# One fp32 product in place of three products of rounded parts, in the time-mixing layer of a hybrid decoder step

## The chip, the cores and the metric

The kernel runs on one core of a Trainium2 chip. The metric is device microseconds of one execution, the median of three runs. The core has five engines with instruction streams of their own: TensorE (PE, whose weight loads are listed apart as PEld), VectorE (DVE), ScalarE (ACT), GpSimd (POOL) and SyncE (SP), which here issues most DMAs.

## The reference, cut to what matters

One inference step of two layers: a Conformer convolution layer and an RWKV-7 time-mixing layer, each followed by a squared-ReLU MLP. 1024 prompt tokens with 16 meta tokens ahead and 8 sampled tokens are computed, all in fp32, with a width of 1024 and 16 heads of 64. The change lies in the time-mixing layer:

```python
prev = concatenate([shift_prev, h[:, :-1]]);  xx = prev - h
xr, xw, xk, xv, xa, xg = (h + xx * x_mix[i] for i in range(6))
r, k, v = xr @ w_r, xk @ w_k, xv @ w_v                       # 1024 x 1024 each
w_log = -softplus(-(w0 + tanh(xw @ w1) @ w2)) - 0.5          # low rank: 64
a = sigmoid(a0 + (xa @ a1) @ a2)                             # low rank: 64
g = sigmoid(xg @ g1) @ g2                                    # low rank: 128
...
S_final, ys = lax.scan(_wkv7_step, S0, (r, decay, k, v, kk, a))
...
out = ((yn + bonus) * g) @ w_o
```

## The kernel before

Activations lie feature-major: 128 features on the partitions, KT = 8 blocks of features, tokens along the free dimension. The time-mixing layer takes the 1048 tokens in four groups (G1: 272, 256, 256 and 264 tokens) through `mixer_in`, while `prepare` of the next group runs between, and the recurrence over 17 chunks of 64 tokens (`chunk`, `front`) is let in piece by piece: `tick` is called at fixed places of the projections and gives the recurrence a credit (`PACE`). The Tile framework then orders the instructions of each engine by priority and by its own simulated times, so the order on an engine is not the order in the code; waits between engines are semaphores.

In a group the phases follow each other: `mixed(0)` makes the mixed input of r (eight tiles `mx`, on VectorE); eight projections of r; `gate`, the first low-rank product of g; the mixed input of k and eight projections of k, each followed by the second low-rank product of g (`lora2`, tile `l_g`) and a column of the norms of kk (`pn`); `decay_rate`, the first low-rank product of w and a together; the mixed input of v and eight projections of v, each with the second low-rank products of w and a (`l_w`, `l_a`), the cumulated decays (`cum`, part of the tile `wa`), the operands of the recurrence (`ab`) and, one tile later, `finish`, which stores `ab`, transposes v and makes the small products `nn` and `pk`.

Every one of these matrix products is made of three: both operands are split into a rounded part of type fp32r and the rest, and `mm3` adds high x high, low x high and high x low in PSUM:

```python
nc.tensor.matmul(ps, w[0], act[0], start=first, stop=False)   # L187
nc.tensor.matmul(ps, w[1], act[0], start=False, stop=False)   # L188
nc.tensor.matmul(ps, w[0], act[1], start=False, stop=last)    # L189
```

The weights come by DMA as columns of 128 (512 KB, `load_raw`, L146, on SyncE's queue). `load_w` casts them on ScalarE (`*_hi`, L157) and subtracts on VectorE (r, k and the first two of v) or on GpSimd (the rest of v, and the low-rank weights) (`*_lo`, L162). `col_stream` holds the order of the 96 columns of r, k and v: loads two columns ahead, the split one ahead. Activations are split by `split` (L140 on ScalarE, L141 on VectorE or GpSimd): `mx` into `mh` and `ml`, the input of the low-rank products `hx` into `hxh` and `hxl` (`input_parts`, let in beside the projections of r), the results of the first low-rank stage into `lgh`, `lgl` and the like. The first low-rank stage (`narrow`) has two weight blocks for each block of features, one for the token's own row and one for the row before it; in the last group the sampled tokens' rows before, `sps`, are put between the others.

The MLPs, the convolution layer's products and w_o use `mm3` as well and are not touched. Some products of the recurrence and its preparation take plain fp32 operands: `A` (L1209), `pk` (L1064), `pn` (L983) and others.

Of the kernel before, what the change touches and what calls it, by code (L numbers as in the profile page):

```python
# [16 lines left out]
P = 128  # L17
# [5 lines left out]
DEC = 8  # L23
# [25 lines left out]
def hybrid_step(tc, x_prompt, x_sample, state_conv, state_shift, state_wkv, meta_tokens,  # L49
# [10 lines left out]
    with ctx:  # L60
        def pool(stack, name, bufs, **kw):
            return stack.enter_context(tc.tile_pool(name=name, bufs=bufs, reuse_waits="tile", **kw))
# [699 lines left out]
        open_ep(ld, 1, "d")  # L762


        lwa = [[lorap.tile([P, N1], F32R, name=f"l{b}{q}") for q in "hl"] for b in "wa"]
        for i in range(2):
            for t in lwa[i]:
                nc.scalar.copy(t[HALF[1 - i]], hsel[HALF[1 - i], 0:1].broadcast_to([HS, N1]))

        prep = {}  # L770
        VSLOW = 0.5
        LO_R = LO_K = lambda p: nc.vector
        LO_V = lambda p: nc.vector if p < 2 else nc.gpsimd

        def prepare(g):

# [32 lines left out]

            def mix(i, k):  # L810

                t = tt(nm("mx", i, k), "t2")
                nc.vector.scalar_tensor_tensor(t[:, :n], xx[:, k, :n], vec("x_mix", i * KT + k), hx[:, k, 1:1 + n],
                                               op0=ALU.mult, op1=ALU.add)
# [6 lines left out]
        RAW_AHEAD, SPLIT_AHEAD = 2, 1  # L821
        wrkv = col_stream([(w, p, f"w{s}{g}_{p}", lo(p)) for g in range(4)
                           for s, w, lo in (("r", rwkv_w_r[0], LO_R), ("k", rwkv_w_k[0], LO_K), ("v", rwkv_w_v[0], LO_V))
                           for p in range(KT)], RAW_AHEAD, SPLIT_AHEAD)
        carry = {"tail": lambda: None}

        def mixer_in(g, tick, ahead):
# [34 lines left out]
            nl = n if npr == n else npr + 2 * DEC  # L862
            HK = KT // 2
            hxs = {}

            def input_parts():
                yield
                for hf in range(2):
                    hi = pr.tile([P, 5 * 4 * HS], F32R, name=nm("hxh", hf), tag="ab", bufs=2)
                    los = [pr.tile([P, 3 * N1], F32R, name=nm("hxl", hf, i), tag=tag, bufs=2) for i, tag in enumerate(("rk2", "wa"))]  # L870
                    for k in range(hf * HK, hf * HK + HK):
                        h_ = hi[:, k % HK * (1 + N1):(k % HK + 1) * (1 + N1)]
                        l_ = los[k % HK // 2][:, k % 2 * (1 + N1):(k % 2 + 1) * (1 + N1)]
                        srcs = [(slice(0, 1 + npr), hx[:, k, :1 + npr])]
                        if npr < n:
                            srcs += [(slice(1 + npr, 1 + nl, 2), sps[:, k]), (slice(2 + npr, 1 + nl, 2), hx[:, k, 1 + npr:1 + n])]
                        for cs, src in srcs:
                            split(h_[:, cs], l_[:, cs], src, nc.gpsimd)
                        hxs[k] = h_, l_
                        if k % 2:  # L880
                            yield

            def narrow_w(i, name):

                return [load_w(d_lr[i, :, hf * HK:(hf + 1) * HK].rearrange("p k s c -> p (k s) c"), (KT, P), nm(name, hf), nc.gpsimd)
                        for hf in range(2)]

            def narrow(ws, name):

                ps = bank(nm("p", name))[:, :nl]  # L890
                for k in range(KT):
                    w = ws[k // HK]
                    for s_ in range(2):
                        j = k % HK * 2 + s_
                        mm3(ps, (w[0][:, j, :], w[1][:, j, :]), [t[:, 1 - s_:1 - s_ + nl] for t in hxs[k]],
                            j == 0 and k == 0, j == KT - 1 and k == KT - 1)
                return ps


            ncols = [(slice(0, npr), slice(0, npr))] + ([(slice(npr, n), slice(npr + 1, nl, 2))] if npr < n else [])  # L900
            lo_ = lambda s: lorap.tile([P, N1], F32R, name=nm(s), tag=s)
            lg = lo_("lgh"), lo_("lgl")
            def decay_rate(ws):
                lf = lorap.tile([P, N1], F32, name=nm("lf"), tag="lf")
                ps = narrow(ws, "wa")
                for d, sc in ncols:
                    nc.scalar.activation(lf[:64, d], ps[:64, sc], AF.Tanh)
                    nc.scalar.copy(lf[64:, d], ps[64:, sc])
                for rows, (hi, lo) in zip(HALF, lwa):
                    split(hi[rows, :n], lo[rows, :n], lf[rows, :n], nc.gpsimd)  # L910

            def gate(ws):
                ps = narrow(ws, "g")
                lf2 = lorap.tile([P, N1], F32, name=nm("lf2"), tag="lf")
                for d, sc in ncols:
                    nc.scalar.activation(lf2[:, d], ps[:, sc], AF.Sigmoid)
                split(lg[0][:, :n], lg[1][:, :n], lf2[:, :n], nc.gpsimd)
# [15 lines left out]

            def second(parts, name):

                raw = cur["raw"].tile([P, D], F32, name=nm(name) + "_raw", tag="raw")
                for rows, src in parts:
                    nc.sync.dma_start(raw[rows], src)
                return load_w(None, (KT, P), nm(name), nc.gpsimd, raw=raw)

            dd = lambda p, i, src: nc.gpsimd.tensor_copy(ddec[:, p, i, :], src)
            allp = slice(0, P)
# [11 lines left out]


            act = mixed(0)
            aside = input_parts()
            both = beside(aside, (0, 1))
            for p in range(KT):
                (both if p else lambda: tick(1.0))()  # L960
                ps = proj(next(wrkv), act, P, f"r{p}", both if p else lambda: tick(1.0))
# [5 lines left out]
                nc.scalar.copy(r[:, :n], ps[:, :n])  # L967
# [5 lines left out]
            for _ in aside:  # L973
                pass
            gate(ws)
            act = mixed(2)
            both = lambda: tick(1.0)
# [23 lines left out]
            r16p = [lorap.tile([P, N1], F32R, name=nm("r16" + q), tag="lg" + q)[:, :n] for q in "hl"]  # L1001

            def norms():
                add_pn()
# [620 lines left out]
```

## Time and profile before

| | |
|---|---|
| median of 3 runs | 2857.89 us (2855.55 to 2860.58) |
| profiled execution, span | 2857.3 us; no other time of it is listed |
| mean granted TensorE clock | 0.961 |
| PE, DVE, ACT, POOL busy | 94%, 69%, 47%, 60% of the span |
| time-mixing projections, first to last matmul | 1126 to 1833 us from the span's start |

Times in the profile are of one execution. Matmuls are pipelined, and the durations of neighbouring ones overlap, so what one costs is read from the step between starts. A product of plain fp32 operands stands in the trace as two records, a product of fp32r operands as one. "Busy" counts the union of the durations. The granted clock (PEclk) is the share of the full TensorE clock that was granted.

### The profile page before, as it was taken

To read this page: it belongs to the slowest core of one execution; us is meant where nothing else is said; L and a number is where in the kernel's file an instruction comes from. 1 tells how busy PE (TensorE), PEld (TensorE's weight loads), DVE (VectorE), ACT (ScalarE), POOL (GpSimd) and SP (SyncE) were. 2 spreads that over 40 slices of the span, in tenths; PEclk is the share of its full clock that TensorE was granted. 3 is DMA by queue.
4 is the path that set the end of the run, shared out by engine and by line. 5 is a ranking of instruction groups with operands and counts; after the bars stand their busy time and mean duration, and the time that the engine had idled before them with its cause. 6 is when DMAs were issued, how large, how long until landed. Compare 5 with 4: busy or idle time off the path is not lost. (4 is left out here: it accounts for less than half of the span.)

```text
span 2857.3 us, 54445 instructions
## 1 busy us (share of the span) xinstructions
PE 2677.4 (94%) x20554; PEld 2557.9 (90%) x20554; DVE 1958.0 (69%) x3726; ACT 1345.6 (47%) x2510; POOL 1703.4 (60%) x2295
## 2 busy tenths in 40 slices
PE   8999999999999899878788899979999999999998
PEld 7989999999999898867787788778889999999998
DVE  5999999995455545478896895689656764443444
ACT  5545444543454334565666857634445552222223
POOL 6676877887788775444543554646448783333332
PEclk9999999999999999988899999989999999999999
DMA  6662544454444642777777968856557742222211
GB/s 179 172 184 85 159 135 133 133 179 140 136 129 148 176 138 91 215 194 198 202 215 208 241 165 198 234 156 159 128 161 213 205 128 85 70 72 67 67 60 41
DMA packets 659285, 428.34 MB, mean 150 GB/s; under 512 B 126840, under 2 KB 609208, under 8 KB 659022
## 3 DMA queue, kind: packets, MB, share of 16 engines
q1 hardware_dynamic: 652780, 421.93, 52.6%
q8 instruction: 162, 2.65, 0.4%
q10 hardware_dynamic: 6018, 2.89, 0.4%
q14 instruction: 101, 0.83, 0.1%
q0 software_dynamic: 224, 0.03, 0.0%
HBM read 353.03 MB, written 72.66 MB: 149 GB/s over the span
## 5 line engine op out<-in xcount | busy, mean ns | idle before, releaser
L162 POOL TENSOR_TENSOR wo_lo<-wo_raw,wo_hi 128x256 fp32r<-128x256 f32 x736 | 561.5, 795 | 300.3 <-ACT wo_hi L157 265.5
L162 POOL TENSOR_TENSOR wi_lo<-wi_raw,wi_hi 128x256 fp32r<-128x256 f32 x640 | 490.4, 797 | 275.5 <-ACT wi_hi L157 264.1
L187 PE MATMUL out<-hh,wo_hi 128*128 128x352 f32 (+2 forms) x1536 | 503.5, 328 | 20.1 <-DVE h L340 10.6
L340 DVE TENSOR_TENSOR h<-h,out 128x352 f32<-128x352 f32 (+2 forms) x768 | 386.3, 510 | 197.8 <-PE out L189 196.9
L187 PE MATMUL ps_in<-m_h,wi_hi 128*128 128x352 f32 (+2 forms) x1536 | 497.4, 324 | 12.2 <-ACT m_h L269 11.5
L189 PE MATMUL out<-hl,wo_hi 128*128 128x352 f32 (+2 forms) x1536 | 496.0, 325 | 4.0 <-DVE hl L141 4.0
L188 PE MATMUL out<-hh,wo_lo 128*128 128x352 f32 (+2 forms) x1536 | 499.4, 325 | 0.0
L188 PE MATMUL ps_in<-m_h,wi_lo 128*128 128x352 f32 (+2 forms) x1536 | 496.5, 324 | 0.0
L189 PE MATMUL ps_in<-m_l,wi_hi 128*128 128x352 f32 (+2 forms) x1536 | 496.2, 323 | 0.1
L504 DVE SCALAR_TENSOR_TENSOR cv<-u,wdw,cv 128x352 f32<-128x352 f32 (+2 forms) x720 | 377.3, 575 | 0.7
L157 ACT CAST wi_hi<-wi_raw 128x1024 fp32r<-128x1024 f32 x160 | 168.1, 1050 | 396.9 <-PE out L189 188.4
L157 ACT CAST wo_hi<-wo_raw 128x1024 fp32r<-128x1024 f32 x184 | 192.9, 1049 | 316.8 <-PE out L189 145.6
L187 PEld LDWEIGHTS out<-hh,wo_hi 128*128 128x128 f32 x1536 | 292.6, 191 | 27.5 <-DVE h L340 14.8
L187 PEld LDWEIGHTS ps_in<-m_h,wi_hi 128*128 128x128 f32 x1536 | 290.6, 189 | 14.6 <-ACT m_h L269 11.6
L189 PEld LDWEIGHTS out<-hl,wo_hi 128*128 128x128 f32 x1536 | 291.6, 190 | 6.4 <-DVE hl L141 5.3
L188 PEld LDWEIGHTS out<-hh,wo_lo 128*128 128x128 f32 x1536 | 292.5, 190 | 1.7
L188 PEld LDWEIGHTS ps_in<-m_h,wi_lo 128*128 128x128 f32 x1536 | 290.3, 189 | 2.0
L189 PEld LDWEIGHTS ps_in<-m_l,wi_hi 128*128 128x128 f32 x1536 | 289.9, 189 | 1.9 <-DVE m_l L270 0.5
L327 DVE SCALAR_TENSOR_TENSOR r<-ps_in,rs_m 128x352 f32<-128x352 f32 (+2 forms) x192 | 98.6, 516 | 232.7 <-PE ps_in L189 228.9
L141 DVE TENSOR_TENSOR hl<-s,hh 128x352 fp32r<-128x352 f32 (+2 forms) x192 | 144.5, 754 | 109.9 <-ACT hh L140 109.8
L329 ACT ACTIVATE s<-r 128x352 f32<-128x352 f32 (+2 forms) x192 | 93.7, 490 | 130.8 <-DVE r L327 130.3
L162 POOL TENSOR_TENSOR wv_lo<-wv_raw,wv_hi 128x256 fp32r<-128x256 f32 x96 | 82.8, 892 | 24.1 <-ACT wv_hi L157 23.8
(402 smaller groups left out, 6155.5 us busy)
## 6 DMA issues: line engine op xcount, KB each, us to landing
wi_raw<-in_w_mlp_in_dram SPq DMA_DIRECT2D x160, 512.0 KB
wo_raw<-in_w_mlp_out_dram SPq DMA_DIRECT2D x160, 512.0 KB
wr_raw<-in_rwkv_w_r_dram SPq DMA_DIRECT2D x32, 512.0 KB
wk_raw<-in_rwkv_w_k_dram SPq DMA_DIRECT2D x32, 512.0 KB
wv_raw<-in_rwkv_w_v_dram SPq DMA_DIRECT2D x32, 512.0 KB
d_ab<-ab SPq DMA_DIRECT2D x32, 512.0 KB
pg_raw<-in_conv_w_pw_dram SPq DMA_DIRECT2D x24, 512.0 KB
pa_raw<-in_conv_w_pw_dram SPq DMA_DIRECT2D x24, 512.0 KB
```

The source lines that it names most:

```text
L141: eng_lo.tensor_sub(lo, src, hi.bitcast(F32))
L157: nc.scalar.copy(hi[:, :a * b], raw[:, :a * b])
L162: eng_lo.tensor_sub(lo[:, cs], raw[:, cs], hi[:, cs].bitcast(F32))
L187: nc.tensor.matmul(ps, w[0], act[0], start=first, stop=False)
L188: nc.tensor.matmul(ps, w[1], act[0], start=False, stop=False)
L189: nc.tensor.matmul(ps, w[0], act[1], start=False, stop=last)
L327: nc.vector.scalar_tensor_tensor(r[:, :n], ps[:, :n], 0.0, rs[:, :n], op0=ALU.max, op1=ALU.mult)
L329: nc.scalar.activation(s[:, :n], r[:, :n], AF.Square)
L340: nc.vector.tensor_add(hv[:, 4 * i + m, :], hv[:, 4 * i + m, :], ps[:, :n])
L504: nc.vector.scalar_tensor_tensor(acc[m][:, :n], ug[:, m, j:j + n], wdw[:, m, j:j + 1], acc[m][:, :n], op0=ALU.mult, op1=ALU.add)
```

## The change

In the time-mixing layer r, k, v and both low-rank stages take the fp32 operands as they are, with one matmul for each product. The casts and subtractions of their weights and activations go, and with them `input_parts` and its places beside r. The weight columns stay in their load buffers until the projection has read them: six buffers, loads four columns ahead. The low-rank weights have a pool of four buffers of their own (`wide`). The mixed inputs are one tile each, from 20 buffers (before: 10 for each part). `narrow` reads `hx` directly, shifted by one column for the second weight block, and adds a product of 8 columns for the sampled tokens in the last group. `r16`, the MLPs, the convolution layer and w_o keep their parts.

```diff
-        def col_stream(cols, raw_ahead, split_ahead, tag="w"):
-            raws, parts = {}, {}
+        def blocks_of(raw):
+            return raw.rearrange("p (a b) -> p a b", a=KT)
+        def col_stream(cols, ahead):
+            raws = {}
             for i in range(len(cols)):
-                for j in range(i, min(i + raw_ahead + 1, len(cols))):
+                for j in range(i, min(i + ahead + 1, len(cols))):
                     if j not in raws:
                         raws[j] = load_raw(col_src(*cols[j][:2]), (KT, P), cols[j][2])
-                for j in range(i, min(i + split_ahead + 1, len(cols))):
-                    if j not in parts:
-                        parts[j] = load_w(None, (KT, P), cols[j][2], cols[j][3], tag, raws[j])
-                yield parts[i]
+                yield blocks_of(raws.pop(i))
...
-        open_weights(ld, 3, {"w": 4}, "d")
-        mixp = pool(ld, "mixp", 10)
+        cur["raw"] = pool(ld, "wrawd", 6)
+        wide = pool(ld, "wided", 4)
+        mixp = pool(ld, "mixp", 20)
...
             def mix(i, k):
-                t = tt(nm("mx", i, k), "t2")
+                t = mixp.tile([P, N1], F32, name=nm("mx", i, k), tag="mx")
                 nc.vector.scalar_tensor_tensor(t[:, :n], xx[:, k, :n], vec("x_mix", i * KT + k), hx[:, k, 1:1 + n], ...
-                hi, lo = (mixp.tile([P, N1], F32R, name=nm("m" + q, i, k), tag="m" + q) for q in "hl")
-                split(hi[:, :n], lo[:, :n], t[:, :n], nc.gpsimd if k % 3 else nc.vector)
-                return hi[:, :n], lo[:, :n]
+                return t[:, :n]
...
             def proj(w, act, wid, name, fill=None):
                 ps = bank(nm("p", name))
                 for k in range(KT):
-                    mm3(ps[:wid, :n], (w[0][:, k, :], w[1][:, k, :]), act[k], k == 0, k == KT - 1)
+                    nc.tensor.matmul(ps[:wid, :n], w[:, k, :], act[k], start=k == 0, stop=k == KT - 1)
...
             def narrow(ws, name):
-                ps = bank(nm("p", name))[:, :nl]
+                ps = bank(nm("p", name))[:, :n]
                 for k in range(KT):
-                    w = ws[k // HK]
-                    for s_ in range(2):
-                        j = k % HK * 2 + s_
-                        mm3(ps, (w[0][:, j, :], w[1][:, j, :]), [t[:, 1 - s_:1 - s_ + nl] for t in hxs[k]], ...
+                    w, j = ws[k // HK], k % HK * 2
+                    nc.tensor.matmul(ps, w[:, j, :], hx[:, k, 1:1 + n], start=k == 0, stop=False)
+                    nc.tensor.matmul(ps[:, :npr], w[:, j + 1, :], hx[:, k, :npr], start=False, ...
+                    if npr < n:
+                        nc.tensor.matmul(ps[:, npr:], w[:, j + 1, :], sps[:, k], start=False, stop=k == KT - 1)
...
             def lora2(w, p, act, name):
                 ps = bank(nm("l2", name))
-                mm3(ps[:, :n], (w[0][:, p, :], w[1][:, p, :]), (act[0][:, :n], act[1][:, :n]), True, True)
+                nc.tensor.matmul(ps[:, :n], w[:, p, :], act[:, :n], start=True, stop=True)
...
-            aside = input_parts()
-            both = beside(aside, (0, 1))
+            both = lambda: tick(1.0)
```

More of the change, by code (lines that the diff above doesn't have):

```diff
@@ L762, in hybrid_step @@
         open_ep(ld, 1, "d")
[L765 to L768, printed above, removed]
+        lwa = [lorap.tile([P, N1], F32, name=f"l{b}") for b in "wa"]
+        for i, t in enumerate(lwa):
+            nc.scalar.copy(t[HALF[1 - i]], hsel[HALF[1 - i], 0:1].broadcast_to([HS, N1]))
         prep = {}
         VSLOW = 0.5
-        LO_R = LO_K = lambda p: nc.vector
-        LO_V = lambda p: nc.vector if p < 2 else nc.gpsimd
         def prepare(g):
@@ L859, in proj, with narrow_w @@
                 return ps
-            nl = n if npr == n else npr + 2 * DEC
             HK = KT // 2
-            hxs = {}
-            def input_parts():
-                yield
+            def narrow_w(i, name):
+                out = []
                 for hf in range(2):
[L869 to L881, printed above, removed]
@@ L883, in narrow_w @@
-            def narrow_w(i, name):
-                return [load_w(d_lr[i, :, hf * HK:(hf + 1) * HK].rearrange("p k s c -> p (k s) c"), (KT, P), nm(name, hf), nc.gpsimd)
-                        for hf in range(2)]
+                    raw = wide.tile([P, D], F32, name=nm(name, hf) + "_raw", tag="wide")
+                    nc.sync.dma_start(blocks_of(raw), d_lr[i, :, hf * HK:(hf + 1) * HK].rearrange("p k s c -> p (k s) c"))
+                    out.append(blocks_of(raw))
+                return out
@@ L900, in mixer_in @@
-            ncols = [(slice(0, npr), slice(0, npr))] + ([(slice(npr, n), slice(npr + 1, nl, 2))] if npr < n else [])
-            lo_ = lambda s: lorap.tile([P, N1], F32R, name=nm(s), tag=s)
-            lg = lo_("lgh"), lo_("lgl")
+                    w, j = ws[k // HK], k % HK * 2
+                    nc.tensor.matmul(ps, w[:, j, :], hx[:, k, 1:1 + n], start=k == 0, stop=False)
+                    nc.tensor.matmul(ps[:, :npr], w[:, j + 1, :], hx[:, k, :npr], start=False, stop=k == KT - 1 and npr == n)
@@ L903, in decay_rate @@
+                    if npr < n:
+                        nc.tensor.matmul(ps[:, npr:], w[:, j + 1, :], sps[:, k], start=False, stop=k == KT - 1)
+                return ps
+            lg = lorap.tile([P, N1], F32, name=nm("lg"), tag="lg")
             def decay_rate(ws):
-                lf = lorap.tile([P, N1], F32, name=nm("lf"), tag="lf")
                 ps = narrow(ws, "wa")
-                for d, sc in ncols:
-                    nc.scalar.activation(lf[:64, d], ps[:64, sc], AF.Tanh)
-                    nc.scalar.copy(lf[64:, d], ps[64:, sc])
@@ L909, in decay_rate @@
-                for rows, (hi, lo) in zip(HALF, lwa):
-                    split(hi[rows, :n], lo[rows, :n], lf[rows, :n], nc.gpsimd)
+                nc.scalar.activation(lwa[0][HALF[0], :n], ps[HALF[0]], AF.Tanh)
+                nc.scalar.copy(lwa[1][HALF[1], :n], ps[HALF[1]])
             def gate(ws):
                 ps = narrow(ws, "g")
-                lf2 = lorap.tile([P, N1], F32, name=nm("lf2"), tag="lf")
-                for d, sc in ncols:
-                    nc.scalar.activation(lf2[:, d], ps[:, sc], AF.Sigmoid)
@@ L917, in gate @@
[L917 removed]
+                nc.scalar.activation(lg[:, :n], ps, AF.Sigmoid)
             def lora2(w, p, act, name):
                 ps = bank(nm("l2", name))
[L921 removed]
+                nc.tensor.matmul(ps[:, :n], w[:, p, :], act[:, :n], start=True, stop=True)
                 return ps
@@ L934, in second @@
             def second(parts, name):
-                raw = cur["raw"].tile([P, D], F32, name=nm(name) + "_raw", tag="raw")
+                raw = wide.tile([P, D], F32, name=nm(name) + "_raw", tag="wide")
                 for rows, src in parts:
                     nc.sync.dma_start(raw[rows], src)
-                return load_w(None, (KT, P), nm(name), nc.gpsimd, raw=raw)
+                return blocks_of(raw)
             dd = lambda p, i, src: nc.gpsimd.tensor_copy(ddec[:, p, i, :], src)
@@ L956, in mixer_in @@
             act = mixed(0)
-            aside = input_parts()
-            both = beside(aside, (0, 1))
+            both = lambda: tick(1.0)
             for p in range(KT):
-                (both if p else lambda: tick(1.0))()
-                ps = proj(next(wrkv), act, P, f"r{p}", both if p else lambda: tick(1.0))
+                both()
+                ps = proj(next(wrkv), act, P, f"r{p}", both)
                 if p == 0:
@@ L970, in mixer_in @@
                     dd(p, 4, r[:, npr:n])
-            for _ in aside:
-                pass
             gate(ws)
             act = mixed(2)
-            both = lambda: tick(1.0)
             pn = bank(nm("pn"), "x")
@@ L1000, in mixer_in @@
             r16 = lorap.tile([P, N1], F32, name=nm("r16"), tag="lf")
-            r16p = [lorap.tile([P, N1], F32R, name=nm("r16" + q), tag="lg" + q)[:, :n] for q in "hl"]
+            r16p = [lorap.tile([P, N1], F32R, name=nm("r16" + q), tag="r16" + q)[:, :n] for q in "hl"]
             def norms():
```

9 lines of the change are left out of this document (3 added, 6 removed).

## The prediction

> **What bounds the kernel now.** I read the page's first two parts, then the stretches of the time-mixing stage, then single matmuls in order of time, then the waits of TensorE, then the groups of the instructions that go.
>
> ```profile
> PE 2677.4 (94%) x20554; PEld 2557.9 (90%) x20554; DVE 1958.0 (69%) x3726; ACT 1345.6 (47%) x2510; POOL 1703.4 (60%) x2295
> ...
> PEclk9999999999999999988899999989999999999999
> ```
>
> TensorE is busy 94% of the span, but the change lies wholly in slices 16 to 25, the only ones with a granted clock of 8 tenths among them. I cut that stage at its phases: for each of four token groups a stretch with the r and k projections, gate and low-rank products, and one with the v projection, here called the v phase.
>
> ```profile
> core 0: us, PE busy (x) PEld busy (x) DVE busy (x) ACT busy (x) POOL busy (x), PEclk, DMA share, GB/s
> 1126.00:1833.00 707.00, 610.11 (x6679) 554.91 (x6679) 540.25 (x1017) 439.64 (x1036) 333.34 (x469) 0.93 0.76 202
> 1126.00:1211.00 85.00, 74.64 (x529) 71.46 (x530) 45.14 (x57) 44.95 (x90) 42.76 (x57) 0.94 0.63 187
> 1211.00:1288.00 77.00, 55.01 (x544) 48.88 (x543) 57.40 (x108) 48.94 (x130) 33.12 (x54) 0.82 0.75 201
> 1288.00:1381.00 93.00, 80.80 (x714) 77.09 (x715) 72.65 (x146) 48.23 (x103) 40.80 (x46) 0.91 0.78 205
> 1381.00:1448.00 67.00, 52.39 (x559) 46.15 (x558) 65.95 (x129) 45.40 (x110) 35.24 (x47) 0.87 0.73 203
> ...
> 1768.00:1833.00 65.00, 64.20 (x941) 56.61 (x940) 47.01 (x95) 49.14 (x133) 39.47 (x78) 1.00 0.83 202
> ```
>
> The stage takes 707 us, a quarter of the span. TensorE is idle for 707 - 610 = 97 us of it, and the clock is granted at 0.93, which takes another 0.07 x 707 = 49 us. So up to 146 us lie in this stage that are not matmul streaming at full clock. They are uneven: the first v phase is idle 22 of 77 us at a clock of 0.82, and in the second VectorE is busy 65.95 of 67 us, that is, VectorE bounds it. The last v phase has 0.8 us idle: there TensorE is the bound already. Every microsecond that the change adds to TensorE is paid in full where it is the bound, and is free only as far as it fills these 146 us.
>
> **What the matmuls cost.** Both kinds of product stand side by side in the trace, in two short stretches in order of time (start, duration, line):
>
> ```profile
> 1605.13 0.28 PE L188 MATMUL p_v<-mh,wv_lo 128*128 128x256 f32 x1
> 1605.24 0.28 PE L189 MATMUL p_v<-ml,wv_hi 128*128 128x256 f32 x1
> 1605.36 0.28 PE L187 MATMUL p_v<-mh,wv_hi 128*128 128x256 f32 x1
> ...
> 1607.73 0.28 PE L189 MATMUL p_v<-ml,wv_hi 128*128 128x256 f32 x1
> ...
> 1312.93 0.59 PE L1209 MATMUL A<-xa,bk 128*128 128x256 f32 x2
> 1313.17 0.47 PE L188 MATMUL p_r<-mh,wr_lo 128*128 128x256 f32 x1
> 1313.48 0.59 PE L1209 MATMUL A<-xa,bk 128*128 128x256 f32 x2
> ```
>
> The durations overlap; the steps from start to start count. A product of rounded parts (fp32r) of 256 columns takes 0.118 us (22 steps from the first to the last of these rows, 2.60 us), so three take 0.354. The recurrence's A product takes plain fp32 operands of the same shape with weights of its own for each product: it is two records, and from one pair to the next 0.55 us pass with one fp32r product between, so it takes 0.55 - 0.12 = 0.43. Each product therefore gets dearer by 0.43 - 0.354, about 0.078 us, in place of cheaper.
>
> The Trainium skill, "FP8 and Floating Point Precision", section TensorE Precision Notes, speaks against this change: true fp32 takes four passes through the array. Four steps of 0.118 would be 0.472, 0.118 dearer than three, where the row gives 0.43; the sum goes by the row.
>
> **The sum on TensorE.** The program's order shows one matmul for each product: 768 for r, k and v, 128 for the first low-rank stage, 96 for the second, 992 in place of 2976. At a mean width of 262 columns the difference is 0.078 x 262/256 = 0.080 us, so TensorE gets 79 us more work. Sixteen products of 8 columns come for the sampled tokens' shifted rows, under 0.1 us each: 80 in all. A weight load goes with each record; under the A rows it does not widen the steps, so it costs nothing here.
>
> **What is taken away.** The casts, subtractions and the parts of the input:
>
> ```profile
> L162 DVE TENSOR_TENSOR wr_lo<-wr_raw,wr_hi 128x1024 fp32r<-128x1024 f32 x32 | 41.5, 1309 | 14.2 <-ACT wr_hi L157 14.1
> L162 DVE TENSOR_TENSOR wk_lo<-wk_raw,wk_hi 128x1024 fp32r<-128x1024 f32 x32 | 39.6, 1237 | 28.2 <-ACT wk_hi L157 26.0 <-PE p_k L188 2.1
> L141 DVE TENSOR_TENSOR ml<-mx,mh 128x256 fp32r<-128x256 f32 (+2 forms) x36 | 22.8, 634 | 14.9 <-ACT mh L140 12.6 <-PE U L1293 2.0
> L157 ACT CAST wr_hi<-wr_raw 128x1024 fp32r<-128x1024 f32 x32 | 33.4, 1050 | 16.9 <-DMA wr_raw<-in_rwkv_w_r_dram 13.0 <-PE p_r L189 3.9
> L162 POOL TENSOR_TENSOR wv_lo<-wv_raw,wv_hi 128x256 fp32r<-128x256 f32 x96 | 82.8, 892 | 24.1 <-ACT wv_hi L157 23.8
> L141 POOL TENSOR_TENSOR ml<-mx,mh 128x256 fp32r<-128x256 f32 (+2 forms) x60 | 60.1, 1012 | 29.2 <-ACT mh L140 25.3 <-ACT wc L1109 1.6 <-PE bT L1270 1.2
> L813 DVE SCALAR_TENSOR_TENSOR mx<-xx,pvec,hx 128x256 f32<-128x256 f32 (+2 forms) x96 | 61.4, 662 | 9.6 <-POOL ml L141 9.2
> ...
> L813 DVE SCALAR_TENSOR_TENSOR mx<-xx,pvec,hx x96: 447/493/1699, 1125.2 to 1748.9; 128x256 f32<-128x256 f32 x48, 128x272 f32<-128x272 f32 x24, 128x264 f32<-128x264 f32 x24
> ```
>
> VectorE loses 41.5 + 39.6 + 22.8 and the first two wv_lo of each group (8 x 1.2), together 114 of its 540 us. ScalarE loses a 1.05 us cast for each of 96 columns (101 us) and the casts of activations and low-rank weights. GpSimd loses nearly all it does here. There is a second gain on VectorE: mx has a median of 493 ns, a mean of 662 and a longest of 1699, so it is held up at times, by 96 x 0.169 = 16 us for mx alone. The Trainium skill, "SBUF — State Buffer", section Who interferes with whom, says that a VectorE instruction with two SBUF inputs contends with a GpSimd instruction that reads SBUF; mx reads two tiles while ml and wv_lo run, and its spread agrees. None of this is time by itself: it counts only through TensorE's waits.
>
> ```profile
> PE nn L1048 <- DVE ab L1129: 16.6, 4, 8.4
> PE p_r L187 <- ACT st L967: 6.0, 1, 6.0
> PE l_w L187 <- ACT wa_hi L157: 5.4, 2, 4.1
> PE A L1209 <- DVE fs L1320: 4.9, 5, 1.9
> PE pk L1064 <- ACT vm L1037: 4.1, 2, 3.2
> PE p_r L189 <- DVE ml L141: 3.5, 2, 2.1
> PE p_r L187 <- DVE n L1050: 3.4, 2, 2.3
> PE l_g L187 <- ACT lgh L140: 3.3, 1, 3.3
> PE A L1209 <- DVE nr L1217: 3.3, 2, 2.1
> ...
> PE p_k L189 <- POOL ml L141: 3.0, 2, 2.2
> ```
>
> (us in total, times, longest.) Waits that name a rounded part go with it: wa_hi 5.4, ml 3.5 and 3.0, lgh 3.3, and smaller rows of the same names, 20 us together (an estimate from these). What is late next for them is mx, one VectorE instruction of 0.49 us, and there are 20 of its tiles instead of 10 pairs, so the next projection's mixes no longer wait for the last reader of this one's. Waits of the recurrence's own chain stay: A on fs 4.9 and on nr 3.3, and the like for U and Y, 16 us in all (an estimate). The other 97 - 20 - 16 = 61 us are waits on a VectorE or ScalarE that is late: ab 16.6, st 6.0, vm 4.1, n 3.4. Their bounds are none and all of it. I take two thirds, 41 us: in the second v phase, where VectorE is full, it loses about 5 us of splits and is no longer held by GpSimd's 35 us there, and TensorE's step per tile grows, so that VectorE has longer to be ready; but a chain of dependent steps that ends in ab remains.
>
> So 61 us of 97 idle go, and of the 49 us of clock the same share, 31, as the clock sank where TensorE idled: 0.82 in the stretch with 22 us idle, 1.00 in that with 0.8. A wait that goes also gives back the part of the last matmul's 0.28 us that did not stream, 0.16, for some 25 waits: 4 us. Given back: 96. The sum is 80 - 96 = -16 us.
>
> **Costed at nothing.** Weight loads are the same bytes, on the same queue (SyncE). They now wait for a buffer that a projection releases, not a cast; queued behind such a wait are the stores of r and k, the fetches for the v phase and the recurrence's loads. The loads run four columns ahead with six buffers, at least 4 x 8 x 0.43 = 14 us. If that cover were gone, the nearest row is wr_hi's wait on wr_raw: 13 us. The chunks of the recurrence stand at the same count beside the projections in both orders (10 of 17 before the last v projection), so the stage behind keeps its work.
>
> **The rivals.** *First, slower: the late steps are latency, not load.* If the waits on ab, st, vm and n stay, since they come from chains of dependent instructions rather than from busy engines, only 20 us of idle and 10 of clock come back: 80 - 30 = +50, 2908 us. For it: VectorE is busy only 57.40 of 77 us in the first v phase, and TensorE still waits 22. Against it: the second v phase, full on VectorE. The point from which it decides is that less than 80 us of the 146 come back. *Second, faster by more:* all of the idle time and clock but the recurrence's 16 us comes back, with its clock: 80 - 122 - 8 = -50, 2808 us. For it: VectorE falls from 540 to about 410 of 707 us, GpSimd to almost none. *Third, no change:* 74 to 86 us come back, 2858. *Fourth, the fp32 product takes four full steps:* 992 x 0.118 x 262/256 = 120 us on TensorE, less 96, gives +24, 2882 us; the A rows speak against it. It is the rule of the precision page above that would make it so. That the change does not do what it says is ruled out by the order: one matmul for each product, and no cast of a weight in the stage.
>
> **How the numbers follow.** The span, 2857.3, is 0.6 below the median of the runs, 2857.89, and no other time of the profiled execution is listed; the sum is made against the span and carried to the median: 2858 - 16 = 2842. Chances: the forecast (faster by 6 to 45) 0.46, the second rival 0.10, the third 0.12, the first 0.27, the fourth 0.05. Faster by over 0.2% (6 us, about what a measurement of this kernel can tell from no change): 0.46 + 0.10 = 0.56; within it 0.12; slower 0.32. The likeliest case's own range is 2813 to 2852. The whole range reaches just past the second rival, 2806, and up to about half-way between the fourth rival and the first, 2888; some 0.06 lie below and 0.13 above.
>
> **What would show it.** In the profile after: p_r rows as two records with steps of 0.216 us; TensorE's busy time in the stage up by some 50 to 80 us less what the clock gives; the stage's idle below 45 us and its clock at 0.96 or more; no ml, mh, wa_hi among the waits; mx's mean near its median. If the waits on ab and n stand as before, the first rival holds. If the A-like step is 0.24 us, the fourth. If the stage is shorter and the total is not, something behind it took the gain, and the sum is wrong in a place I left out.

## The result, and the profile after

| | before | after |
|---|---|---|
| median | 2857.91 us (2855.55 to 2860.58) | 2867.97 us (2865.08 to 2873.90) |
| ratio, 95% interval | | 1.0042 [1.0029, 1.0055] |
| profiled execution, and its span | 2857.3 (span) | 2865.08, span 2863.4 |
| granted clock | 0.961 | 0.975 |

The kernel got slower by 0.42%, 10 us, where 16 us of gain were forecast. Each time is the median of five runs. The profiled execution of after is the fastest of its runs; against the span of before it is 6 us longer.

The first part of the page of after, and the clock's slices:

```profile
PE 2756.3 (96%) x19594; PEld 2553.4 (89%) x19594; DVE 1795.2 (63%) x3618; ACT 1185.9 (41%) x2230; POOL 1436.1 (50%) x1983
...
PEclk9999999999999999989999999989999999999999
```

VectorE, ScalarE and GpSimd lost 163, 160 and 267 us of work, and the clock's 8s within the stage (slices 16 to 25) fell from three to one. TensorE's busy time rose by 79 us. Where, the stretches tell: ahead of the stage, the stage (first r matmul to last v matmul), behind it. First of before, then of after:

```profile
core 0: us, PE busy (x) PEld busy (x) DVE busy (x) ACT busy (x) POOL busy (x), PEclk, DMA share, GB/s
0.00:1126.00 1126.00, 1079.39 (x6654) 1063.84 (x6654) 838.36 (x1596) 520.05 (x791) 859.01 (x1179) 0.98 0.50 146
...
1833.00:2857.00 1024.00, 987.95 (x7231) 939.17 (x7222) 579.39 (x1115) 385.92 (x685) 511.06 (x649) 0.97 0.42 119
```

```profile
0.00:1126.00 1126.00, 1079.85 (x6659) 1063.69 (x6660) 842.44 (x1612) 516.21 (x787) 860.72 (x1179) 0.98 0.50 147
1126.00:1842.00 716.00, 688.94 (x5689) 552.27 (x5687) 371.49 (x892) 284.61 (x759) 63.45 (x156) 0.97 0.73 196
1842.00:2863.00 1021.00, 987.50 (x7253) 937.41 (x7252) 581.29 (x1115) 385.06 (x686) 511.90 (x650) 0.97 0.42 119
...
1208.00:1280.00 72.00, 55.86 (x464) 42.65 (x462) 48.20 (x117) 32.98 (x104) 6.11 (x21) 0.89 0.70 202
...
1388.00:1476.00 88.00, 86.11 (x782) 64.64 (x781) 54.12 (x118) 41.38 (x110) 8.73 (x18) 0.92 0.68 184
1785.00:1842.00 57.00, 57.00 (x548) 45.06 (x548) 36.84 (x75) 31.72 (x97) 14.77 (x47) 1.00 0.53 153
```

Ahead of the stage nothing moved between these two executions; behind it 3 us went. The stage itself takes 716 us where it took 707. In it TensorE is idle 27 us (716 - 688.94) where it was 97, the clock is 0.97 where it was 0.93, VectorE fell from 540 to 371 and GpSimd from 333 to 63. So nearly all of what was to be freed was freed, and the stage is longer all the same. Of the phases, the first v phase still idles 16 of 72 us, the second v phase, once bound by VectorE (65.95 of 67 us), now holds TensorE busy for 86.11 of 88 (more of the recurrence stands in it: 782 matmul records, 559 before), and the last has no idle time at all.

The waits of TensorE in the stage of after (total us, times, longest):

```profile
PE pb L740 <- DVE rk L1064: 6.6, 2, 5.6
PE p_r L851 <- DVE n L1017: 4.1, 1, 4.1
PE nn L1015 <- DVE ab L1096: 3.1, 3, 1.9
...
PE nm L1023 <- ACT vm L1004: 1.5, 1, 1.5
```

No `ml`, `mh`, `wa_hi` or DMA is among them; the wait on `ab` fell from 16.6 to 3.1, that on `st` (6.0) is gone. Two did not fall: `p_r` on `n` (3.4 before, 4.1 now) and `pb` on `rk` (3.2 and 6.6).

What the busy time now holds shows in single matmuls in order of time, in a stretch of the third v phase where TensorE never idles (start, duration):

```profile
1584.14 3.62 PE L851 MATMUL p_v<-mx,wv_raw 128*128 128x256 f32 x16
1587.60 0.59 PE L892 MATMUL l_w<-lw,wa_raw 128*128 128x256 f32 x2
...
1590.95 0.44 PE L1214 MATMUL gg<-x,no 32*32 32x32 f32 x16
...
1591.86 1.03 PE L851 MATMUL p_v<-mx,wv_raw 128*128 128x256 f32 x4
1592.81 0.24 PE L1214 MATMUL gg<-x,no 32*32 32x32 f32 x2
1592.98 2.86 PE L851 MATMUL p_v<-mx,wv_raw 128*128 128x256 f32 x12
```

A v projection is 16 records, two for each of eight products. In one piece it takes 3.62 us, so a product takes (3.62 - 0.17) / 8 = 0.43, where 0.17 is the part of the last record that does not stream: the price of the A rows. In the second case two 32x32 records of the recurrence stand between, and from 1591.86 to 1595.84 it takes 3.98 us: two tiny records cost 0.36 us, while sixteen of them in one piece take 0.44. What costs is the change between products that use the whole array (`128*128`) and products that use a part of it (`32*32`), there and back.

I counted this over the stage. Each matmul's step, from the end of the one before to its own end, is compared with its step in undisturbed rows (118 ns for a product of parts and 216 ns for a record of a plain fp32 product, at 256 columns; 28 to 52 ns for the small ones). The sum of these is called streaming. What a step has beyond that is put under changes where the array shape differs from that of the matmul before, the clock is full and the excess lies between 60 and 250 ns; all else, idle time and lowered clock included, is other waits. The changes are a firm count: with each shape's median step as the undisturbed one they come to 33 us (199) and 62 us (386). The other two columns move by about 12 us with that choice.

| us in the stage | length | streaming | changes (number) | other waits |
|---|---|---|---|---|
| before | 707 | 512 | 32 (198) | 163 |
| after | 716 | 597 | 61 (387) | 58 |

One change costs 0.157 us (60.6 / 387; 0.159 before), and there are twice as many. Steps without a change of shape have next to no excess: in after 2274 of them exceed by 2.8 us in all, and 34 more by 3.6. The order of the program says the same without a trace: up to the last v projection 244 changes of shape in before, 420 in after, with 10 of the 17 chunks of the recurrence in both. The recurrence is not moved; it is cut into finer pieces between the projections. Behind the stage there are 310 and 303.

Two sums that need no such sorting agree. The clock was halved for 106 us of the stage in before, of which TensorE was busy 83, and for 41 in after, of which it was busy 36; so 41 and 18 us of its busy time were lost. Busy time less this loss rose from 569 to 671 us, by 102. The records of the projections and low-rank products themselves, each step counted up to the median of its kind, rose from 357 to 440 us, by 83. So at least 19 us of busy time were added that are not these products, where the count above has 29 for the changes.

The Trainium skill, "TensorEngine Tiling (Array Packing)", section Tiling Modes, says that changing the tiling mode, rather than just the tile, drains TensorE. The trace agrees so far as a delay is seen at such a change, 0.157 us a time; a drain as such has no row in it.

### The profile page after: what moved, and what is told of

It is laid out like the page before. It is cut to its first block, busy times and chain, and to the rows that moved or that the text cites. A ratio compares the mean times of both kernels' runs of the same rounds, so it can differ in the third digit from the quotient of the medians.

```text
span 2863.4 us, 51601 instructions
## 1 busy us (share of the span) xinstructions
PE 2756.3 (96%) x19594; PEld 2553.4 (89%) x19594; DVE 1795.2 (63%) x3618; ACT 1185.9 (41%) x2230; POOL 1436.1 (50%) x1983
## 3 DMA queue, kind: packets, MB, share of 16 engines
q10 hardware_dynamic: 6018, 2.89, 0.4%
## 4 chain that ended last, share of the span: by engine, by line
PE 37%; DVE 7%; POOL 5%; DMA 3%; issue 3%; ACT 1%; SPq 0%; DVEq 0%; POOLq 0%; ACTq 0%
PE ps_in L187 3%; PE ps_in L188 3%; PE ps_in L189 3%; POOL wo_lo L162 3%; PE out L187 3%; PE out L189 3%; PE out L188 3%; PE p_v L851 3%; PE p_k L851 2%; POOL wi_lo L162 2%; PE p_r L851 2%; PE A L1176 2%; DVE ni L1136 1%; DVE tt L1135 1%; PE U L1260 1%
## 5 line engine op out<-in xcount | busy, mean ns | idle before, releaser
L851 PE MATMUL p_r<-mx,wr_raw 128*128 128x256 f32 (+2 forms) x512 | 123.4, 396 | 4.1 <-DVE n L1017 4.1
```

The source lines that it names most:

```text
L851: nc.tensor.matmul(ps[:wid, :n], w[:, k, :], act[k], start=k == 0, stop=k == KT - 1)
```

## The experiments

Two theories stood against each other. S: the waits came back as forecast and more, and the gain went into changes of array shape. P: the price of the products is simply paid in full, and the order is of no account. Beside them stood the prediction's first rival, late steps that are latency (L below). Each kernel ran on one chip beside runs of before of its own, and its ratio is to those; the chips are not all the same.

**The recurrence's priority raised throughout, in both kernels.** `RC` is the priority offset that the recurrence's instructions get; raised, the scheduler holds them together.

```diff
-        RC = 0
+        RC = 1000
```

> The changed kernel with one number altered: the recurrence's instructions get a priority 1000 places higher (RC = 1000 in place of 0), so that the scheduler lets each of its steps run in one piece. In the order of TensorE's instructions the changes between matmuls of different array shape (full 128x128 against 32, 64 and 128x64 tiles) fall from 420 to 316 up to the last v projection and from 303 to 74 behind it. Theory S (a change of shape costs TensorE 0.157 us, and the changed kernel's shortfall is 193 more of them, 460 against 267 by the trace): 333 fewer, up to -52 us, so 2816 to 2840 us. Theory P (the shortfall is the price of the fp32 products, paid in full where TensorE is the bound, and the order does not matter): 2868 us, within 6.

> The kernel before with the same one number (RC = 1000). Changes of shape rise from 244 to 287 in the stage and fall from 310 to 93 behind it. Theory S: +7 - 34 = -27 us where TensorE is the bound, so about 2831 us, and the changed kernel with the same number is 0 to 20 us below it. Theory P: 2858 us, and the changed kernel with the same number 10 us above it.

After with this edit: 2848.86 us against 2855.39, ratio 0.9974 [0.9960, 0.9988], by the ratios about 20 us below after, between what S (2816 to 2840) and P (2868) said. Before with it: 2854.60, ratio 0.9997 [0.9987, 1.0007], where S expected 27 us of gain and P none. In both the program's changes fell most behind the stage (303 to 74, and 310 to 93). In before that is 217 changes or 34 us by the price above, less 43 more in the stage (7 us), and it won nothing. So a count of changes times a price is not what an order is worth. Where the gain went is not shown by the stage alone, for the edit also moves work: 208 records of the recurrence's `A` stand in the stage in place of 172, the stage of before grows from 707 to 761 us (its other waits from 163 to 189), and the stretch behind it shrinks from 1024 to 972.

**The price by itself.** The two dense layers, with no recurrence beside them, got one small matmul in the middle of each of 288 products: of 32x32, or of the whole array with 32 columns, both reading the identity.

```diff
                 mm3(ps[:, :n], ...)
+                if k == KT // 2 - 1:
+                    nc.tensor.matmul(ps[:32, 448:480], ident[:32, :32], ident[:32, :32], start=False, stop=False, ...)   # dense_small
+                    nc.tensor.matmul(ps[:, 448:480], ident, ident[:, :32], start=False, stop=False)                      # dense_full
```

> The kernel before with one more matmul in the middle of each of the 288 dense products of the MLPs, the convolution layer and w_o, where TensorE is busy throughout: a 32x32 tile with 32 columns into unused columns of the same bank (its result is not read). Theory S: two changes of shape at each place, 288 x 0.31 = 90 us, and some 10 for the matmul: about 2955 us. Theory P gives a small matmul no more than a larger one: no more than the companion run with a full 128x128 matmul of 32 columns.

> The companion: a full 128x128 plain fp32 matmul of 32 columns at the same 288 places, so no change of shape. Both theories: two records of 0.03 to 0.11 us each, 17 to 63 us, so 2875 to 2921 us; theory S says at least 30 us below the run with the small one.

With 32x32: 2943.79 us, ratio 1.0310 [1.0279, 1.0341], 88 us for 288 places, 0.31 us each. The matmul's own two records are some 0.05 of it (sixteen in a row took 0.44), which leaves about 0.13 for each of the two changes, a little under the 0.157 of the stage. With the whole array: 2918.42, ratio 1.0217 [1.0196, 1.0239], 63 us, 0.22 each. In order of time, first the 32x32, then the whole array:

```profile
2551.37 0.32 PE L188 MATMUL ps_in<-m_h,wi_lo 128*128 128x352 f32 x1
2551.53 0.32 PE L189 MATMUL ps_in<-m_l,wi_hi 128*128 128x352 f32 x1
2551.78 0.24 PE L199 MATMUL ps_in<-ident 32*32 32x32 f32 x2
2551.96 0.43 PE L187 MATMUL ps_in<-m_h,wi_hi 128*128 128x352 f32 x1
2552.22 0.32 PE L188 MATMUL ps_in<-m_h,wi_lo 128*128 128x352 f32 x1
```

```profile
2500.56 0.32 PE L189 MATMUL ps_in<-m_l,wi_hi 128*128 128x352 f32 x1
2500.72 0.30 PE L199 MATMUL ps_in<-ident 128*128 128x32 f32 x2
2500.86 0.41 PE L187 MATMUL ps_in<-m_h,wi_hi 128*128 128x352 f32 x1
2501.10 0.32 PE L188 MATMUL ps_in<-m_h,wi_lo 128*128 128x352 f32 x1
```

The usual step is 0.16 us. The 32x32 matmul starts 0.25 after the one before it: it waits 0.09 more before it can begin. That of the whole array starts on time, and pays only behind. The comparison separates less than was expected (25 us, at least 30 were asked for): a short matmul of the whole array is dear too. Against P the small one is still the dearer by 25 us. That the price of 0.31 is one of the change of shape alone is thus not shown by this pair; that the places cost that much is, and that steps between full-width products don't carry it is shown by the 2274 steps above.

**Cheap products, nothing split.** Three bf16 products of the operands' upper halves stand in for each fp32 product. They stream nearly as the products of parts did, and nothing needs to be made for them.

```diff
+        def three(ps, w, act, first, last):
+            w, act = (t.bitcast(BF16)[:, 1::2] for t in (w, act))
+            for i in range(3):
+                nc.tensor.matmul(ps, w, act, start=first and i == 0, stop=last and i == 2)
...
-                    nc.tensor.matmul(ps[:wid, :n], w[:, k, :], act[k], start=k == 0, stop=k == KT - 1)
+                    three(ps[:wid, :n], w[:, k, :], act[k], k == 0, k == KT - 1)
```

> The changed kernel with its 992 fp32 products replaced by three bf16 products each, of the high halves of the same tiles as they land (nothing is split; the result is not that of the reference). So the splits are gone as in the changed kernel, but TensorE has about 992 x 3 x 0.11 = 327 us of these products instead of 432. Theory P (the price of the fp32 products is paid nearly in full): 75 to 105 us below the changed kernel, 2765 to 2795 us, which is also what the taken-away splits are worth by themselves: 60 to 90 us below the kernel before. Theory L (the stage is held by chains of waits that are latency): no more than 40 us below the changed kernel, 2830 us or more.

2793.15 us against 2859.94, ratio 0.9769 [0.9754, 0.9784]: 67 us below before, and by the ratios 78 us below after. Its stage:

```profile
1124.00:1772.00 648.00, 588.15 (x6707) 462.05 (x6705) 371.00 (x893) 283.13 (x759) 65.26 (x153) 0.94 0.82 217
```

One of its v projections in one piece:

```profile
1529.76 2.89 PE L188 MATMUL p_v<-mx,wv_raw 128*128 128x256 bf16 x24
```

This is what P expected (at most 2795 us); L, which asked for 2830 or more, is false. VectorE and GpSimd are as busy as in after (371 and 65 us). The products are not quite those of before: a bf16 product of 256 columns steps by 0.114 us (23 steps and a last record of 0.28 in these 2.89), one of parts by 0.118, so that the rows of the products come to 346 us where before has 357. Of the 67 us some 10 may thus be the products' own, and freeing the side engines is worth 57 to 67 (an estimate). The stage counts as 508 streaming, 44 in 329 changes, 96 other waits. From here to after streaming grows by 89 us (by the rows of the products alone, 93), of which 78 are paid. In the stage, of the 89 the waits absorb 38, 17 more go into changes, and it grows by 68.

**Parts for some projections alone.** If the price is paid in full, parts must pay where they cost little. In these kernels the named projections are split again (by ScalarE and VectorE, none by GpSimd); all others, and both low-rank stages, take single fp32 products.

```diff
+                for j in range(i, min(i + 2, len(cols))):
+                    if j not in parts and cols[j][2][1] in 'rk':      # 'k', or 'rkv', in the others
+                        parts[j] = load_w(None, (KT, P), cols[j][2], nc.vector, "w", raws[j])
...
+                if parts:
+                    split(hi[:, :n], lo[:, :n], t[:, :n], nc.vector)
```

> Part of the change: r and k go back to three products of rounded parts (split on VectorE), v and both low-rank stages keep the single fp32 products: 480 dearer products instead of 992, 38 us more on TensorE than before. Buffers differ too, for lack of memory: four for weight columns and three for low-rank weights. Changes of shape in the stage are 257 in TensorE's order, nearly the 244 of before (420 in the changed kernel). Theory S (changes of shape made the shortfall): the waits given back, some 40 to 50 us, now outweigh the products: 2840 to 2856 us. Theory P: half of the changed kernel's loss, 2860 us.

> The same with the recurrence's priority raised (RC = 1000): 297 changes of shape in the stage and 76 behind. From the changed kernel with that priority (0.9974 of before) 512 products fall by 0.08 us, 41 us, if the splits of r and k stay beside TensorE's work: 2810 to 2835 us. If the splits hold TensorE up again: 2850 us.

> The same with k alone in parts: 256 products fall by 0.08 us from the changed kernel with raised priority, 20 us: 2825 to 2845 us; 2850 us if the splits hold TensorE up.

> The other part of the change: r, k and v as three products of rounded parts (split on VectorE), both low-rank stages with single fp32 products: 224 dearer products, 18 us more on TensorE. The input's parts and the low-rank weights' splits go, and with them the waits on wa_hi and lgh, some 10 to 15 us with the clock; all splits that stay are on VectorE, which held the second v phase before. Both theories: -5 to +20 us, 0.998 to 1.007 of before; S adds 35 changes of shape in the stage (279 against 244), 5 us, P none.

| | median, us | ratio, 95% interval |
|---|---|---|
| r and k in parts | 2832.29 | 0.9906 [0.9887, 0.9925] |
| the same, priority raised | 2831.45 | 0.9899 [0.9881, 0.9917] |
| k in parts, priority raised | 2830.71 | 0.9901 [0.9886, 0.9916] |
| r, k and v in parts (low rank alone single) | 2849.82 | 0.9968 [0.9956, 0.9980] |

The first three lie about 1% below before, and can't be told apart. The first and the last came out better than either theory had them. With the priority raised, k alone takes off 21 us for 256 products, as priced (20); r and k together take off 21 as well, where 41 were priced, so there r in parts brought nothing. The stage of the first:

```profile
1120.00:1814.00 694.00, 636.68 (x6228) 550.78 (x6231) 471.16 (x1039) 366.62 (x890) 64.29 (x156) 0.95 0.77 204
```

552 streaming, 36 in 224 changes, 106 other waits. Streaming is 45 us less than in after, for 512 products at 0.08 (41). Changes are 25 less, and the other waits are 48 more. GpSimd stays at 64 us, as no split is left to it.

**The order undone inside the stage alone.** The priority is raised up to the last v projection and dropped behind it, so the tail keeps its order (316 changes in the program, 303 in after).

```diff
+        st['rc'] = 1000
+        rec = ranked(lambda: st['rc'], recurrence())
...
             mixer_in(g, ...)
+        st['rc'] = 0
```

> The changed kernel again, to stand beside the others on the same chip: 1.004 of before, as measured, by both theories.

> The changed kernel with the recurrence's priority raised inside the time-mixing stage alone (1000 places, and 0 again behind it), so that the rest of the order stays: changes of shape 292 in place of 420 in the stage, 316 in place of 303 behind it, ten chunks of the recurrence in the stage as before. Theory S: 115 fewer x 0.157 = -18 us, some of it lost in waits: 0.998 of before (0.997 to 1.001). Theory P: 1.004, as the changed kernel.

> k in parts, the rest single, and the priority raised inside the stage alone: 292 changes of shape in the stage, 316 behind. From the run with the raised priority in the stage, 256 products fall by 0.08 us: -20 us, 0.991 of before (0.988 to 0.996).

After, run again on this chip: 2872.98 against 2859.34, ratio 1.0047 [1.0035, 1.0060]. With the stage's order undone: 2862.35, ratio 1.0015 [1.0002, 1.0027], 9 us less by the ratios. P expected nothing (1.004) and S 18 less some waits (at most 1.001): the run lies between, outside both. Its waits show where the rest may have stayed:

```profile
PE pb L740 <- DVE rk L1064: 8.1, 3, 5.6
PE yn L1397 <- DVE ey L1393: 4.7, 2, 4.1
PE A L1176 <- DVE fs L1287: 4.1, 1, 4.1
```

Changes fell from 61 to 43 us (387 to 272), but waits over 1 us rose from 26 to 46: `A` waits for `fs` again, 4.1 us in place of 0.7, and `yn` for `ey`, which was not among after's waits. Against the execution of after that was profiled on the same chip, changes fell by 16 us (60 to 43) and other waits rose by 14 (69 to 83). These two executions took 2874.58 and 2873.47 us, so the 9 us rest on the medians, and the trace does not show them. With k in parts on top: 2846.86, ratio 0.9961 [0.9949, 0.9973], 15 us below the last for 256 products, where 256 x 0.08 is 20.

## Why the prediction was wrong

The forecast was -16 us and the profiled pair gave +6, a miss of 22 (the medians gave +10); the time lay inside the range, but the sign was the other one. The signs that the prediction named for its case came true: two records with steps of 0.216 us, 27 us of idle time, a clock of 0.97, no `ml`, `mh` or `wa_hi` among the waits, `mx` at its median. None of them could show what was missing, save one: TensorE's busy time rose by 79 us, where 80 less what the clock gave back, 23 to 28, should have stood. Term by term:

**The products: right, but for the smallest.** p_r's records step by 0.216 us, 0.43 a product. Streaming in the stage rose by 85 us (597 - 512) where 80 were forecast. About half of these 5 are the sixteen products of 8 columns, which were put at under 0.1 us each, without a row that says so. Here is one round of the first low-rank stage:

```profile
1716.95 0.28 PE L875 MATMUL p_g<-sps,g_raw 128*128 128x8 f32 x2
1717.09 0.69 PE L872 MATMUL p_g<-hx,g_raw 128*128 128x264 f32 x2
1717.62 0.59 PE L873 MATMUL p_g<-hx,g_raw 128*128 128x256 f32 x2
1718.05 0.28 PE L875 MATMUL p_g<-sps,g_raw 128*128 128x8 f32 x2
```

The round takes 1.10 us; less the 0.446 and 0.432 of its two wide products (two steps of 0.223 and of 0.216), 0.22 stay for the product of 8 columns, 3.5 us for sixteen. The fourth rival is false: it put a product at four steps of 0.118, 0.472, and the uninterrupted projection shows 0.43. The Trainium skill, "FP8 and Floating Point Precision", section TensorE Precision Notes, says that true fp32 takes four passes; the trace does not speak against that number, as four of 0.108 make 0.43. What was wrong in the rival is to take a step of the parts for the length of a pass.

**What comes back: right in size.** Forecast were 61 us of idle time, 31 of clock, 4 of tails, 96 together. Idle time gave 70 (97 to 27), the clock 28 by the same reckoning (49 to 0.03 x 716 = 21). That reckoning is 8 us too high for before, since the clock was low in idle time too and only 41 us were lost from busy time; so taken, the clock gave 23. In the count other waits fell by 105 (163 to 58), 9 more than forecast. The first rival, that the late steps are latency, is false in the main: the wait on `ab` fell from 16.6 to 3.1 us, though those of `p_r` on `n` and of `pb` on `rk` stayed. VectorE was no longer held up, as the prediction said of `mx`:

```profile
L811 DVE SCALAR_TENSOR_TENSOR mx<-xx,pvec,hx x96: 452/482/502, 1110.6 to 1712.9; 128x256 f32<-128x256 f32 x48, 128x272 f32<-128x272 f32 x24, 128x264 f32<-128x264 f32 x24
```

Its longest fell from 1699 to 502 ns. The Trainium skill, "SBUF — State Buffer", section Who interferes with whom, says that a VectorE instruction with two SBUF inputs contends with a GpSimd instruction that reads SBUF; the trace agrees, with GpSimd busy for 63 us of the stage in place of 333. This gain of `mx`, 16 us, was in the forecast. That VectorE came out even below it (371 against some 410 us) is for the most part due to steps that the change does not touch. `tt` and `ni`, the matrix inversions of the recurrence, went from 422 and 433 ns to 342 and 339, 21 us together (before, then after):

```profile
L1169 DVE TENSOR_TENSOR ni<-ni,tt 128x30 f32<-128x30 f32 (+29 forms) x120 | 51.9, 433 | 2.3
L1168 DVE TENSOR_TENSOR tt<-ni 128x30 f32<-128x30 f32 (+29 forms) x120 | 50.6, 422 | 9.4 <-DMA ni<-d_n 7.3
```

```profile
L1135 DVE TENSOR_TENSOR tt<-ni 128x30 f32<-128x30 f32 (+29 forms) x120 | 41.0, 342 | 23.9 <-DMA ni<-d_n 20.5
L1136 DVE TENSOR_TENSOR ni<-ni,tt 128x30 f32<-128x30 f32 (+29 forms) x120 | 40.6, 339 | 3.3
```

That it is GpSimd's work that mattered, and not VectorE's own load, is borne out by the kernel with r, k and v in parts, all split on VectorE: VectorE is busy 517 us of its stage, GpSimd 70, and `tt` and `ni` take 334 and 341 ns.

**The step that failed: what was costed at nothing.** The prediction said that the recurrence's chunks stand at the same count beside the projections in both orders, and so took the work around the change as unchanged. The count is the same, 10, and the stage behind did keep its work (3 us less). But the order inside the stage was compared by that count alone, and its grain was not looked at: 244 changes of array shape in the program became 420, and in the trace they take 29 us more (198 to 387). This term was missing. With it the sum is 85 + 29 - 105 = +9 in the stage, less 3 behind: +6. What could be seen ahead was all there: the two orders, and the price, in any stretch of the trace of before where a projection is cut by a small product:

```profile
1661.02 0.28 PE L188 MATMUL p_r<-mh,wr_lo 128*128 128x264 f32 x1
1661.23 0.24 PE L1247 MATMUL gg<-x,no 32*32 32x32 f32 x2
1661.40 0.39 PE L189 MATMUL p_r<-ml,wr_hi 128*128 128x264 f32 x1
1661.64 0.28 PE L187 MATMUL p_r<-mh,wr_hi 128*128 128x264 f32 x1
```

From the first to the last start 0.62 us pass, where two steps of 0.12 would do: 0.38 for two records of 32x32.

How far the changes alone are the cause is only partly settled. Shown are their number, their place and the price of a place (0.31 us with a small matmul in a dense layer). Lessened inside the stage, they gave 9 us back by the medians (the intervals of the two ratios allow some 4 to 14), not the whole 18 that their fall was worth, and in the profiled pair the coarser order waited longer by nearly as much. So the missing 29 and the 9 that the waits gave above the forecast are partly one thing: a fine order buys short waits with changes. A kernel with after's products in exactly before's order was not tried.

**Loads.** That the weights' DMA loads are covered was right: no DMA is among TensorE's waits in the stage.

**A slip** in reading the page: the prediction named slices 16 to 25 as the only ones with an 8 in the clock's line of before, but one more stands in that line, just behind the stage.

**The weighing.** The third rival, no change, with 74 to 86 us given back, was the closest in number, by luck: net of the changes 76 came back, but no rival had the changes in it. The prediction took the 146 us of idle time and clock as what TensorE's work could sink into. The kernel with cheap products shows that 57 to 67 us are to be had from freeing the side engines, and that most of what a product then gets dearer is paid (78 of some 90 us), as TensorE has little idle time left by then (27 us of 716 in after).

## What to carry to other kernels

Cut such a change in two before summing it: what freeing the side engines is worth at unchanged products, and what dearer products cost once TensorE has become the bound, which here was most of their price. A mix can beat both ends: r and k in parts, v and the low-rank stages single, took 1% less than before. Why it does is only argued (the side engines have room for those splits); k alone in parts with the priority raised did as well, and v alone in parts was not tried. And where a scheduler decides the order on the bound engine, compare the grain of the two orders, not only what stands before what: here 176 more changes of array shape came with an edit that touched none of the small products.

## What the runs showed of the hardware that was not expected

- A change between matmuls that use the whole array and such that use a part of it takes 0.157 us (387 of them in after); in a dense layer one 32x32 matmul with the changes around it took 0.31 us. Small records of one shape in a row take about 0.03 (sixteen of 32x32 in 0.44 us).
- One short fp32 matmul of the whole array, 32 columns wide, between longer products costs 0.22 us (63 us for 288), though its two records stream only 64 columns. One of 8 columns costs the same 0.22 (the round of 1.10 us in after).
- Taking GpSimd's work away shortened VectorE instructions that the change does not touch, in the mean: 422 to 342 ns for `tt`, 433 to 339 for `ni`. They stay short (334 and 341) where VectorE is busy 517 us of the stage and GpSimd only 70.
- A bf16 product of 256 columns steps by 0.114 us (the kernel with cheap products), an fp32r product by 0.118 (before).
